# A conditioning projection moved to plain float32 matmuls in 32-column groups, beside a sample attention that has them

## The chip, the cores and the metric

The kernel is one program on one core of a Trainium2 chip. The time is device microseconds of one execution; the figure of merit is the median of several runs. A profiled execution gives the trace.

The engines by their short names: PE is TensorE, whose weight loads are listed apart as PEld; DVE is VectorE, ACT is ScalarE, POOL is GpSimd, and SP is SyncE, which here only issues DMAs, in the order of its queue.

## The reference

One layer of a hybrid encoder for two request groups with shared weights: a prompt of 1024 tokens and 8 samples of 16 tokens each, all float32, width 1024.

```python
def _adaln(c, w_ada, b_ada):                      # w_ada: 1024 x 9216
    return jnp.split(jax.nn.silu(c) @ w_ada + b_ada, 9, axis=-1)

def _layer(x, c, mixer_fn, w_ada, b_ada, ...):
    sh1, sc1, gt1, sh2, sc2, gt2, sh3, sc3, gt3 = _adaln(c, w_ada, b_ada)
    x = x + 0.5 * gt1[:, None, :] * _swiglu(_modulate(x, g_ffn1, sh1, sc1), w_up1, w_down1)
    m, states = mixer_fn(_modulate(x, g_mix, sh2, sc2))
    x = x + gt2[:, None, :] * m
    x = x + 0.5 * gt3[:, None, :] * _swiglu(_modulate(x, g_ffn2, sh3, sc3), w_up2, w_down2)
    return _rms(x, g_final), states
```

`_modulate(x, g, shift, scale)` is `_rms(x, g) * (1 + scale) + shift`; `_swiglu` has an inner width of 2816. The mixer projects to q, k, v, forget logits and a convolution pair, runs a forgetting attention on 8 heads of 64 (the samples with 256 cached keys each) and a causal convolution of 31 taps, and projects back. The conditioning vectors `c` are few: one for the prompt and eight for the samples, so `_adaln` is a product of 9 x 1024 by 1024 x 9216. Its nine results (shift, scale and gate of three sublayers) are what the change is about.

## The kernel before, in words

All 1152 tokens are kept transposed in SBUF (features on the 128 partitions, tokens along the free axis), in three chunks of 384 tokens; chunk 2 holds the samples in its last 128 columns.

Numbers of float32 go through PE split in two: a value rounded to `float32r` (hi) and the rest (lo), and `mm3` makes three matmuls of them (hi·hi, hi·lo, lo·hi; lines 478 to 480). The weights come as blocks of 512 KB through `Stream` (`ws`): SP loads a block (`raw`, three buffers), ACT rounds it (`wh`, L117), POOL or DVE subtracts (`wl`, L118).

PE's order is written by hand: within `manual_schedule` its instructions run in the order of the program. The other engines' order, and that of SP's queue, is the planner's.

`ffn` goes over units: U (up: two matmul groups `ua` and `ub` of 24 matmuls in `glu_mm`, then the SwiGLU on ACT and DVE) and D (down: eight groups `d`). Each unit runs over the three chunks. `tick()` is called after `ua`, after `ub` and after each half of a down; what was put off with `defer(n, f)` runs n ticks later. In this way small pieces of work are placed between the matmuls of the FFN.

The conditioning is one of them. `w_ada` is taken as 18 column blocks j of 512 (block j is half of one of the nine results); each has 8 steps of 128 rows (k). The stationary operand is the conditioning (9 vectors), the moving one the rows of `w_ada` (128 x 512), and the result (9 x 512) collects in a PSUM bank `pa`. When a block is complete, ACT copies it out (`ev`, L355), `ada_tail` transposes it in four pieces to feature layout (`pt`), and DVE adds the bias (`mods`, L365) and prepares scale and gate (`finish_mod`).

- Blocks are computed in the order 2, 0, 3, 1, 4, 5, 6, ..., 17 (`ADA_ORDER`): first halves of scale and shift of the first FFN, then the second halves, the gate, and then the rest.
- The first two blocks are plain float32 matmuls (L348, stationary operand `cst32`, 9 columns wide). The other 16 are split: ACT rounds 128 x 512 (`ahi`, L335), DVE or POOL subtracts (`alo`, L336), and two matmuls (L351 and L352) use an 18 column wide stationary operand `cst` with the hi and lo parts of the conditioning side by side. The two results of 9 rows are added on DVE (L368).
- Rows come by `ada_load` (256 KB each, three buffers `araw`), and for the first four blocks six of eight k in one load of 1.5 MB (`ada_bulk`), into room that the normalised input `hh`/`hl` takes later.
- The first two blocks run ahead of the FFN. The FFN then starts with chunk 0 on half of its features, in four banks `ub` side by side; `first(k)` is called between its pieces. `first(1)` transposes the x of chunk 1 into place, `first(4)` runs blocks three and four and the norm of the second half, `first(5)` and `first(6)` the norm statistics of chunk 1 (`stats_b`: `nb`, L429) and its normalisation, `first(7)` places chunk 2, and `first(9)` starts `ada_tick`, which from then on makes one step each tick (two for a stretch of blocks six and seven).
- PSUM has eight banks; in this part of the kernel one pool of eight serves all of it, `pa` too.

The sample attention later in the kernel already has plain float32 matmuls in 32-column groups: `s_b` (L1054, bank `sS`) and `s_d` (L1077, `sO`) put four small products in the four 32-partition groups of one bank:

```python
for p in range(4):
    rows = slice(32 * p, 32 * p + 32)
    pe.matmul(b[rows, :LK], lhsT=bd[:, rows], rhs=KT[:, p, :], start=True, stop=False)
```

Of the kernel before, what the change touches and what calls it, by code (L numbers as in the profile page):

```python
# [17 lines left out]
P = 128  # L18
D = 1024
KD = D // P  # L20
# [23 lines left out]
def trunk_layer(  # L44
# [18 lines left out]
    const = ctx.enter_context(tc.tile_pool(name="const", bufs=1, side="left"))  # L63
# [14 lines left out]
    def defer(n, f):  # L78
        pending.append([n, f])
# [49 lines left out]
    def kpn(ap):  # L129
        return ap.rearrange("(k p) n -> p k n", p=P)  # L130
# [53 lines left out]
    mods = const.tile([P, 72, 9], F32, name="mods")  # L184
    amod = const.tile([P, 3, KD, 9], F32, name="amod")
    hgate = const.tile([P, 2, KD, 9], F32, name="hgate")
    cst = const.tile([P, KD, 18], F32R, name="cst")
    xt = [xp.tile([P, KD, C], F32, name=f"x{c}") for c in range(NC3)]
    bada = vecs[:, 0:72]
    gnorm = [vecs[:, 72 + 8 * i:80 + 8 * i] for i in range(3)]  # L190
# [6 lines left out]
    nfsd = dram.tile([H, NS, LK], F32, name="nfsd")  # L197

    mps, ps = open_pool("ps", "left", space=PSUM)
    nb = 8  # L200

    def bank(name="b"):
        return ps.tile([P, 512], F32, tag="b", name=name, bufs=nb)
# [15 lines left out]
    cst32 = pro.tile([P, KD, 9], F32, tag="cst32", name="cst32")  # L219
    xin = {}  # L220

    def load_x(i):
# [28 lines left out]
    def T(out, in_):  # L251
        pe.transpose(out, in_, ident[:in_.shape[0], :in_.shape[0]])
# [3 lines left out]
    for k in range(KD):  # L256
        T(pc[:, k * 9:(k + 1) * 9], cwide[:, k * P:(k + 1) * P])
    pcv = pc[:, :72].rearrange("p (k s) -> p k s", s=9)
    act.copy(cst[:, :, 0:9], pcv)
    dve.tensor_copy(cst32, pcv)  # L260
    dve.tensor_sub(cst[:, :, 9:18], pcv, r32(cst[:, :, 0:9]))

    def place_vec():
        pv = bank("pv")
        T(pv[:, :80], vrow)
        act.copy(vecs[:, :80], pv[:, :80])
# [18 lines left out]
                dve.tensor_copy(dst, src)  # L285


    ADA_ORDER = [2, 0, 3, 1, 4, 5] + list(range(6, 18))
# [12 lines left out]
    KORD = [6, 7, 0, 1, 2, 3, 4, 5]  # L301

    def ada_load(n):
        if n < 18 * KD and n not in ada_raw:
            j, k = ADA_ORDER[n // KD], KORD[n % KD]
            t = adp.tile([P, 512], F32, tag="araw", name="araw", bufs=3)
            sp.dma_start(t, w_ada[0, k * P:(k + 1) * P, j * 512:(j + 1) * 512])
            ada_raw[n] = t

    def ada_bulk(g, tag):  # L310
        j = ADA_ORDER[g]
        for n in range(g * KD, g * KD + 2):
            ada_load(n)
        t = hp.tile([P, 6, 512], F32, tag=tag, name="abulk")
        sp.dma_start(t, kpn(w_ada[0, :6 * P, j * 512:(j + 1) * 512]))
        for k in range(6):
            ada_raw[g * KD + 2 + k] = t[:, k]

    FULL = 2
    NA = 18 * KD  # L320
    ada_q, ada_t, ada_n, ada_p = [], [], [0], [None]

    def ada_split():
        n = ada_n[0]
        ada_n[0] += 1
        if n >= 4 * KD - 2:
            for q in range(max(n, 4 * KD), n + 3):
                ada_load(q)
        raw = ada_raw.pop(n)
        if n < FULL * KD:  # L330
            ada_q.append((n, raw, None))
            return
        hi = adp.tile([P, 512], F32R, tag="ahi", name="ahi", bufs=3)
        lo = adp.tile([P, 512], F32R, tag="alo", name="alo", bufs=3)
        act.copy(hi, raw)  # L335
        (pool_e if n >= 4 * KD else dve).tensor_sub(lo, raw, r32(hi))  # L336
        ada_q.append((n, hi, lo))

    def ada_mm():
        n, hi, lo = ada_q.pop(0)  # L340
        j, k = ADA_ORDER[n // KD], KORD[n % KD]
        first, last = n % KD == 0, n % KD == KD - 1
        if first:
            ada_p[0] = bank("pa")
        pa = ada_p[0]
        if lo is None:
            r = 9
            pe.matmul(pa[:r, :], lhsT=cst32[:, k, :], rhs=hi, start=first, stop=last)  # L348
        else:
            r = 18  # L350
            pe.matmul(pa[:r, :], lhsT=cst[:, k, :], rhs=hi, start=first, stop=False)  # L351
            pe.matmul(pa[:r, :], lhsT=cst[:, k, :], rhs=lo, start=False, stop=last)  # L352
        if last:
            ev = tmp(512, "ev", r)
            act.copy(ev, pa[:r, :])  # L355
            ada_t.append((j, r, ev))

    def ada_tail():
        j, r, ev = ada_t.pop(0)
# [3 lines left out]
        ptv = pt[:, :4 * r].rearrange("p (i s) -> p i s", s=r)  # L363
        dst = mods[:, 4 * j:4 * j + 4, :]
        dve.tensor_tensor(  # L365
            dst, ptv[:, :, 0:9], bada[:, 4 * j:4 * j + 4].unsqueeze(2).to_broadcast([P, 4, 9]), ALU.add)
        if r == 18:
            dve.tensor_tensor(dst, ptv[:, :, 9:18], dst, ALU.add)  # L368
        finish_mod(j)

    def ada_step():
        if ada_t:
            ada_tail()
        if ada_n[0] < NA:
            ada_split()
            if len(ada_q) > 2:
                ada_mm()
        elif ada_q:
            ada_mm()
        return ada_n[0] < NA or ada_q or ada_t  # L380

    def ada_blocks(n):
        for _ in range(n):
            ada_split()
            if len(ada_q) > 1:
                ada_mm()

    def ada_close():
        while ada_q:
            ada_mm()  # L390
        ada_tail()

    def ada_group():
        ada_blocks(KD)
        while ada_q:
            ada_mm()

    def run(gen, n):
# [188 lines left out]
            after(c)  # L587


    ada_bulk(0, "hh1")  # L590
    ada_bulk(1, "hl1")
    for i in range(3):
        place_x(i, xin[i])
    stats_a(0)
# [8 lines left out]
    ada_tail()  # L603
# [17 lines left out]
    def first(k):  # L621
        if k == 0:
            norm_apply(0, 0, (0, 1))
        elif k == 1:
            for i in range(3, 6):
                place_x(i, xin[i])
        elif k == 4:
            ada_blocks(KD + 2)
            ada_tail()
            ada_blocks(KD - 2)  # L630
            ada_close()
            norm_apply(0, 0, (2, 3))
            stats_a(1)
        elif k == 5:
            stats_b(1)
        elif k == 6:
            stats_c(1)
            norm_apply(1, 0)
        elif k == 7:
            for i in range(3):  # L640
                place_x(6 + i, x2[:, i])
        elif k == KD + 1:
            load_small()
            ada_tick()
# [28 lines left out]
    mps, ps = open_pool("ps1", "left", space=PSUM)  # L673
    nb = 6
# [186 lines left out]
    for cb, (c0, n) in enumerate(QKV):  # L861
# [3 lines left out]
        for tt in [8] + list(range(8)):  # L865
# [10 lines left out]
            rows = slice(tt * P, (tt + 1) * P)  # L876
            t = sample_rows(cb) if tt == 8 and cb > 1 else tmp(256, "qkv")
# [359 lines left out]
    for n in range(len(stages) + LAG):  # L1237
        q = {k: [] for k in "SBXY"}
        if n < len(stages):
            h, j = stages[n]  # L1240
# [9 lines left out]
        if n >= LAG:  # L1250
            h, j = stages[n - LAG]
# [14 lines left out]
    mps, ps = open_pool("ps3", "left", space=PSUM)  # L1266
    nb = 8
# [23 lines left out]
    mh, hp = open_pool("h2", "left")  # L1291
# [98 lines left out]
```

## Time and profile before

| | |
|---|---|
| median of 3 runs | 2399.08 us (2397.36 to 2401.82) |
| profiled execution, its own time | 2399.03 us |
| its span in the trace | 2397.3 us |
| mean granted PE clock | 0.989 |
| instructions | 34979 |

How to read the profile. Busy time of an engine counts its work, not its waits or the issuing of DMAs. Matmuls are pipelined: a record's length runs from its start to the end of its results, so that lengths overlap and the distance from start to start says what one costs. In the timeline a row is a run of like instructions: start, length from the first start to the last end, engine, line, operation, out<-in, stationary and moving shapes, and in brackets the idle time before it and what ended it. In the table of stretches each row is a part of the span. The rows of a tile give the shortest, middle and longest duration in ns, then the first and the last start.

### The profile page before, as it was taken

How to read it: one execution, taken by the hardware profiler on the slowest of the kernel's cores; microseconds unless marked ns; L12 is line 12 of the kernel's file. 1: busy time of each engine (PE TensorE's matmuls, PEld its weight loads, DVE VectorE, ACT ScalarE, POOL GpSimd, SP SyncE). 2: the span in 40 equal slices, each digit the busy share in tenths (PEclk: the TensorE clock that was granted, in tenths of full speed). 3: DMA queues.
4: the chain of work that ended last, by engine and by line, in shares of the span. 5: the costliest groups of instructions: out<-in, count | busy, mean ns of one | idle time of the engine just before them, and what ended most of it. 6: DMA issues, size and time to landing. Idle time of an engine off the chain costs nothing.

```text
span 2397.3 us, 34979 instructions
## 1 busy us (share of the span) xinstructions
PE 2335.4 (97%) x13971; PEld 2236.0 (93%) x13971; DVE 1277.2 (53%) x2381; ACT 729.5 (30%) x1567; POOL 680.8 (28%) x535
## 2 busy tenths in 40 slices
PE   8899999999999999999989999999999999999998
PEld 4899999999999999999987779999999999999997
DVE  5542543343344436799978887744442344333345
ACT  5533222222111113412658764431111111111112
POOL 2254444443211211131536651112112121121220
PEclk9899999999999999999999999999999999999999
DMA  8133333332111111114233331111111111111102
GB/s 296 57 115 96 95 94 99 93 89 66 45 44 36 47 42 36 37 54 140 89 94 126 93 96 36 45 36 51 38 36 53 36 45 44 36 53 36 37 26 79
DMA packets 176699, 165.81 MB, mean 69 GB/s; under 512 B 11135, under 2 KB 143147, under 8 KB 176529
## 3 DMA queue, kind: packets, MB, share of 16 engines
q1 hardware_dynamic: 176537, 163.58, 22.5%
q8 instruction: 110, 1.80, 0.3%
q14 instruction: 52, 0.43, 0.1%
HBM read 147.10 MB, written 16.68 MB: 68 GB/s over the span
## 4 chain that ended last, share of the span: by engine, by line
PE 84%; DVE 10%; ACT 2%; DMA 2%; issue 1%; POOL 0%; SPq 0%; DVEq 0%; ACTq 0%; POOLq 0%
PE ub L479 8%; PE ub L478 8%; PE ub L480 8%; PE ua L479 8%; PE ua L480 8%; PE ua L478 8%; PE d L480 8%; PE d L478 8%; PE d L479 8%; DVE cv L728 4%; DVE acc L729 1%; DMA nfb<-nfd 1%; PE pa L351 1%; PE pa L352 1%; PE wo L480 1%
## 5 line engine op out<-in xcount | busy, mean ns | idle before, releaser
L118 POOL TENSOR_TENSOR wl<-raw,wh 128x1024 fp32r<-128x1024 f32 (+1 forms) x152 | 368.5, 2432 | 1246.3 <-ACT wh L117 1237.9
L517 DVE TENSOR_TENSOR g<-ub,sg 128x384 f32<-128x384 f32 x132 | 73.6, 558 | 764.5 <-PE ub L480 735.8
L478 PE MATMUL ub<-hh,wh 128*128 128x384 f32 x1168 | 397.7, 341 | 2.5 <-ACT hh L462 2.5
L479 PE MATMUL ub<-hl,wh 128*128 128x384 f32 x1168 | 397.5, 340 | 1.9 <-DVE hl L463 1.9
L480 PE MATMUL ub<-hh,wl 128*128 128x384 f32 x1168 | 397.0, 340 | 0.0
L478 PE MATMUL ua<-hh,wh 128*128 128x384 f32 x1136 | 382.0, 336 | 3.7 <-ACT hh L473 3.3
L479 PE MATMUL ua<-hl,wh 128*128 128x384 f32 x1136 | 381.7, 336 | 0.2
L480 PE MATMUL ua<-hh,wl 128*128 128x384 f32 x1136 | 381.3, 336 | 0.0
L485 DVE SCALAR_TENSOR_TENSOR x<-d,hgate,x 128x384 f32<-128x384 f32 (+1 forms) x528 | 296.1, 571 | 134.0 <-PE d L480 127.9
L117 ACT CAST wh<-raw 128x1024 fp32r<-128x1024 f32 (+1 forms) x160 | 165.6, 1050 | 652.4 <-issue 332.6
L478 PE MATMUL d<-gh,wh 128*128 128x384 f32 x1056 | 357.7, 339 | 3.7 <-DVE t L461 3.6
L480 PE MATMUL d<-gh,wl 128*128 128x384 f32 x1056 | 358.1, 339 | 0.0
L479 PE MATMUL d<-gl,wh 128*128 128x384 f32 x1056 | 357.3, 338 | 0.0
L478 PEld LDWEIGHTS ub<-hh,wh 128*128 128x128 f32 x1168 | 221.2, 189 | 7.6 <-ACT hh L462 2.7
L479 PEld LDWEIGHTS ub<-hl,wh 128*128 128x128 f32 x1168 | 221.2, 189 | 4.3 <-DVE hl L463 2.7
L478 PEld LDWEIGHTS ua<-hh,wh 128*128 128x128 f32 x1136 | 214.4, 189 | 9.5 <-ACT hh L473 4.4
L480 PEld LDWEIGHTS ub<-hh,wl 128*128 128x128 f32 x1168 | 221.2, 189 | 0.0
L479 PEld LDWEIGHTS ua<-hl,wh 128*128 128x128 f32 x1136 | 214.3, 189 | 2.9 <-DVE hl L474 1.0
L336 POOL TENSOR_TENSOR alo<-araw,ahi 128x512 fp32r<-128x512 f32 x112 | 149.0, 1335 | 237.2 <-ACT ahi L335 237.2
L480 PEld LDWEIGHTS ua<-hh,wl 128*128 128x128 f32 x1136 | 214.4, 189 | 0.0
L478 PEld LDWEIGHTS d<-gh,wh 128*128 128x128 f32 x1056 | 199.4, 189 | 8.8 <-DVE t L461 3.9
L521 DVE TENSOR_TENSOR gl<-g,gh 128x384 fp32r<-128x384 f32 x132 | 164.6, 1247 | 68.8 <-ACT gh L520 68.8
(274 smaller groups left out, 3634.8 us busy)
## 6 DMA issues: line engine op xcount, KB each, us to landing
raw<-in_w_up_dram SPq DMA_DIRECT2D x88, 512.0 KB
araw<-in_w_ada_dram SPq DMA_DIRECT2D x120, 256.0 KB
raw<-in_w_down_dram SPq DMA_DIRECT2D x44, 512.0 KB
raw<-in_w_in_dram SPq DMA_DIRECT2D x18, 512.0 KB
abulk<-in_w_ada_dram SPq DMA_DIRECT2D x4, 1536.0 KB
out_dram<-yo SPq DMA_DIRECT2D x18, 256.0 KB
out_dram<-qkv SPq DMA_DIRECT2D x34, 128.0 KB
room<-in_cache_k_dram SPq DMA_DIRECT2D x8, 512.0 KB
```

What stands on the lines that cost most here:

```text
L117: act.copy(hi[:, :a * b], raw)
L118: self.sub.tensor_sub(lo[:, :a * b], raw, r32(hi[:, :a * b]))
L336: (pool_e if n >= 4 * KD else dve).tensor_sub(lo, raw, r32(hi))
L351: pe.matmul(pa[:r, :], lhsT=cst[:, k, :], rhs=hi, start=first, stop=False)
L352: pe.matmul(pa[:r, :], lhsT=cst[:, k, :], rhs=lo, start=False, stop=last)
L478: pe.matmul(out, lhsT=wh, rhs=mh_, start=first, stop=False)
L479: pe.matmul(out, lhsT=wh, rhs=ml_, start=False, stop=False)
L480: pe.matmul(out, lhsT=wl, rhs=mh_, start=False, stop=last)
L485: dve.scalar_tensor_tensor(xs[:, :n], b[:, :n], gate[:, dt, 0:1], xs[:, :n], ALU.mult, ALU.add)
L517: dve.tensor_tensor(g32, pb[:, :C], sg, ALU.mult)
L521: dve.tensor_sub(gl[:, cs], g32, r32(gh[:, cs]))
L728: dve.scalar_tensor_tensor(cv if j < CW - 1 else acc[ct][:, :SEQ], u0, w, cv, ALU.mult, ALU.add)
```

## The change

- All of the conditioning becomes plain float32. The split operand `cst`, the rounding and the subtraction (`ada_split`) and the second addition go.
- The stationary operand `cst32` is 32 columns wide: the nine vectors, and zeros.
- Column blocks are computed in sets: two sets of two blocks, one of two (the gate) and three of four (`SETS`). A step takes one k for all blocks of its set; block i of the set writes partitions 32i to 32i+31 of `pa`. There are 6 x 8 = 48 steps in place of 144.
- `pa` gets a bank of its own, and the pool keeps seven.
- A load brings the rows of the whole set: 128 x 1024 or 128 x 2048 (the first two sets, whose blocks aren't next to each other, by two loads), with two buffers. `ada_step`, `ada_blocks` and `ada_close` go.
- At the start, two steps of set 0 run ahead of the vector transposes and `stats_b`, and six behind them. `first(4)` runs set 1. `ada_tick` makes one step each tick for set 2 and the first step of each set, and otherwise one each fourth tick.
- `ada_tail` transposes 64 or 128 rows in four pieces, once for a set.

```diff
-    cst = const.tile([P, KD, 18], F32R, name="cst")
-    nb = 8
+    nb = 7
...
+    cst32 = adp.tile([P, KD, 32], F32, tag="cst32", name="cst32")
-    act.copy(cst[:, :, 0:9], pcv)
-    dve.tensor_copy(cst32, pcv)
-    dve.tensor_sub(cst[:, :, 9:18], pcv, r32(cst[:, :, 0:9]))
+    dve.memset(cst32, 0.0)
+    dve.tensor_copy(cst32[:, :, 0:9], pcv)
...
+    SETS = [[2, 0], [3, 1], [4, 5]] + [list(range(j, j + 4)) for j in range(6, 18, 4)]
+    STEPS = [(s, k) for s in range(len(SETS)) for k in KORD]
     def ada_load(n):
-            t = adp.tile([P, 512], F32, tag="araw", name="araw", bufs=3)
-            sp.dma_start(t, w_ada[0, k * P:(k + 1) * P, j * 512:(j + 1) * 512])
+        t = adp.tile([P, 2048], F32, tag="araw", name="araw", bufs=2)
+        if js == list(range(js[0], js[0] + len(js))):
+            sp.dma_start(t[:, :512 * len(js)], rows[:, 512 * js[0]:512 * (js[-1] + 1)])
+        else:
+            for i, j in enumerate(js):
+                sp.dma_start(t[:, 512 * i:512 * (i + 1)], rows[:, 512 * j:512 * (j + 1)])
...
     def ada_mm():
+            ada_p[0] = ps.tile([P, 512], F32, tag="pa", name="pa", bufs=1)
-            pe.matmul(pa[:r, :], lhsT=cst[:, k, :], rhs=hi, start=first, stop=False)
-            pe.matmul(pa[:r, :], lhsT=cst[:, k, :], rhs=lo, start=False, stop=last)
+        for i, raw in enumerate(ada_raw.pop(n)):
+            pe.matmul(pa[32 * i:32 * i + 32, :], lhsT=cst32[:, k, :], rhs=raw, start=first, stop=last)
+        if n >= 2 * KD - 2:
+            ada_load(n + 2)
         if last:
-            ev = tmp(512, "ev", r)
-            act.copy(ev, pa[:r, :])
+            ev = tmp(512, "ev", 32 * len(js))
+            act.copy(ev, pa[:32 * len(js), :])
...
-    ada_group()
+    for _ in range(2):
+        ada_mm()
     place_vec()
     stats_b(0)
-    ada_tail()
-    ada_group()
+    for _ in range(6):
+        ada_mm()
     stats_c(0)
     ada_tail()
     ws.split(2)
-    ada_bulk(2, "hh2")
-    ada_bulk(3, "hl2")
+    ada_bulk(1, ("hh2", "hl2"))
...
         elif k == 4:
-            ada_blocks(KD + 2)
+            ada_group()
             ada_tail()
-            ada_blocks(KD - 2)
-            ada_close()
...
     def ada_tick():
-        if 5 * KD <= ada_n[0] < 6 * KD + 4:
-            ada_step()
-        if ada_step():
+        if ada_ev:
+            ada_tail()
+        if ada_n[0] < len(STEPS):
+            ada_mm()
+            defer(1 if ada_n[0] < 3 * KD or ada_n[0] % KD == 0 else 4, ada_tick)
+        elif ada_ev:
             defer(1, ada_tick)
```

More of the change, by code (lines that the diff above doesn't have):

```diff
@@ L218, in trunk_layer @@
     vrow2 = adp.tile([28, P], F32, tag="vrow2", name="vrow2")
-    cst32 = pro.tile([P, KD, 9], F32, tag="cst32", name="cst32")
     xin = {}
@@ L285, in place_x @@
                 dve.tensor_copy(dst, src)
-    ADA_ORDER = [2, 0, 3, 1, 4, 5] + list(range(6, 18))
+    SETS = [[2, 0], [3, 1], [4, 5]] + [list(range(j, j + 4)) for j in range(6, 18, 4)]
+    KORD = [6, 7, 0, 1, 2, 3, 4, 5]
+    STEPS = [(s, k) for s in range(len(SETS)) for k in KORD]
     def finish_mod(j):
@@ L300, in trunk_layer @@
     ada_raw = {}
-    KORD = [6, 7, 0, 1, 2, 3, 4, 5]
     def ada_load(n):
-        if n < 18 * KD and n not in ada_raw:
-            j, k = ADA_ORDER[n // KD], KORD[n % KD]
-            t = adp.tile([P, 512], F32, tag="araw", name="araw", bufs=3)
-            sp.dma_start(t, w_ada[0, k * P:(k + 1) * P, j * 512:(j + 1) * 512])
-            ada_raw[n] = t
-    def ada_bulk(g, tag):
-        j = ADA_ORDER[g]
+        if n >= len(STEPS) or n in ada_raw:
+            return
+        g, k = STEPS[n]
@@ new lines, in ada_load @@
+        js = SETS[g]
+        t = adp.tile([P, 2048], F32, tag="araw", name="araw", bufs=2)
+        rows = w_ada[0, k * P:(k + 1) * P]
+        if js == list(range(js[0], js[0] + len(js))):
[3 more added lines that the diff above has]
+                sp.dma_start(t[:, 512 * i:512 * (i + 1)], rows[:, 512 * j:512 * (j + 1)])
+        ada_raw[n] = [t[:, 512 * i:512 * (i + 1)] for i in range(len(js))]
@@ L312, in ada_bulk @@
+    def ada_bulk(g, tags):
         for n in range(g * KD, g * KD + 2):
             ada_load(n)
-        t = hp.tile([P, 6, 512], F32, tag=tag, name="abulk")
-        sp.dma_start(t, kpn(w_ada[0, :6 * P, j * 512:(j + 1) * 512]))
-        for k in range(6):
[L317 to L323, printed above, removed]
+        ts = []
+        for j, tag in zip(SETS[g], tags):
+            t = hp.tile([P, 6, 512], F32, tag=tag, name="abulk")
+            sp.dma_start(t, kpn(w_ada[0, :6 * P, j * 512:(j + 1) * 512]))
+            ts.append(t)
+        for k in range(6):
+            ada_raw[g * KD + 2 + k] = [t[:, k] for t in ts]
@@ L324, in ada_split, with ada_mm @@
+    ada_n, ada_p, ada_ev = [0], [None], []
+    def ada_mm():
         n = ada_n[0]
         ada_n[0] += 1
[L326 to L341, printed above, removed]
+        g, k = STEPS[n]
+        js = SETS[g]
         first, last = n % KD == 0, n % KD == KD - 1
         if first:
-            ada_p[0] = bank("pa")
+            ada_p[0] = ps.tile([P, 512], F32, tag="pa", name="pa", bufs=1)
         pa = ada_p[0]
[L346 to L352, printed above, removed]
+        for i, raw in enumerate(ada_raw.pop(n)):
+            pe.matmul(pa[32 * i:32 * i + 32, :], lhsT=cst32[:, k, :], rhs=raw, start=first, stop=last)
@@ L353, in ada_mm @@
+        if n >= 2 * KD - 2:
+            ada_load(n + 2)
         if last:
-            ev = tmp(512, "ev", r)
-            act.copy(ev, pa[:r, :])
-            ada_t.append((j, r, ev))
+            ev = tmp(512, "ev", 32 * len(js))
+            act.copy(ev, pa[:32 * len(js), :])
+            ada_ev.append((js, ev))
     def ada_tail():
-        j, r, ev = ada_t.pop(0)
+        js, ev = ada_ev.pop(0)
+        r = 32 * len(js)
         pt = bank("pt")
@@ L362, in ada_tail @@
             T(pt[:, i * r:(i + 1) * r], ev[:, i * P:(i + 1) * P])
[L363 to L372, printed above, removed]
-            ada_tail()
[L374 to L391, printed above, removed]
+        for i, j in enumerate(js):
+            ptv = pt[:, :4 * r].rearrange("p (i s) -> p i s", s=r)[:, :, 32 * i:32 * i + 9]
+            dve.tensor_tensor(
+                mods[:, 4 * j:4 * j + 4, :], ptv, bada[:, 4 * j:4 * j + 4].unsqueeze(2).to_broadcast([P, 4, 9]),
+                ALU.add)
+            finish_mod(j)
     def ada_group():
-        ada_blocks(KD)
-        while ada_q:
+        for _ in range(KD):
             ada_mm()
@@ L587, in ffn @@
             after(c)
-    ada_bulk(0, "hh1")
-    ada_bulk(1, "hl1")
+    ada_bulk(0, ("hh1", "hl1"))
     for i in range(3):
@@ L599, in trunk_layer @@
     ws.dma(3)
-    ada_group()
+    for _ in range(2):
+        ada_mm()
     place_vec()
     stats_b(0)
-    ada_tail()
-    ada_group()
+    for _ in range(6):
+        ada_mm()
     stats_c(0)
```

## Prediction

> **What bounds the kernel now.** The page first: which engine is full.
>
> ```profile
> span 2397.3 us, 34979 instructions
> ...
> PE 2335.4 (97%) x13971; PEld 2236.0 (93%) x13971; DVE 1277.2 (53%) x2381; ACT 729.5 (30%) x1567; POOL 680.8 (28%) x535
> ```
>
> TensorE (PE) is busy for 97% of the span. An average hides stages, so next comes the table of stretches over the part in which the conditioning runs. Its columns: length, then busy time (and instructions) of PE, weight loads, VectorE, ScalarE, GpSimd, then granted clock, DMA share and GB/s.
>
> ```profile
> 62.00:130.00 68.00, 63.31 (x329) 57.69 (x329) 37.13 (x67) 37.65 (x68) 22.88 (x14) 0.90 0.25 74
> 130.00:600.00 470.00, 470.00 (x2639) 440.86 (x2638) 189.90 (x321) 123.88 (x211) 208.12 (x132) 1.00 0.31 91
> 600.00:800.00 200.00, 200.00 (x1147) 200.00 (x1146) 74.35 (x133) 32.55 (x50) 38.41 (x16) 1.00 0.14 43
> ```
>
> From 130 to 600 us PE has no idle time at all, at full clock. Whatever time an instruction holds PE there is time of the kernel, and GpSimd (208 us) and ScalarE (124 us) are cover only. Ahead of 130 us PE does wait, so the two regions are costed apart: the steady part by PE time, the front by its waits. Then the rows that touch the conditioning's accumulator pa:
>
> ```profile
> L351 PE MATMUL pa<-ahi,cst x128: 387/395/408, 41.8 to 591.8; 128*18 128x512 f32 x128
> ...
> L348 PE MATMUL pa<-abulk,cst x24: 592/592/597, 13.6 to 26.4; 128*9 128x512 f32 x24
> ...
> L348 PE MATMUL pa<-araw,cst x8: 592/592/597, 11.7 to 21.3; 128*9 128x512 f32 x8
> ```
>
> L351 has 128 executions, and L352 as many beside it: 16 column blocks x 8 k, a hi and a lo matmul each. The first two blocks are plain float32 (L348). There the trace shows 24+8 records for 2 x 8 matmuls, so a plain float32 matmul is two records.
>
> **Steady part, what goes.** The matmul timeline around 200 us (start, length, ...):
>
> ```profile
> 200.17 0.40 PE L351 MATMUL pa<-ahi,cst 128*18 128x512 f32 x1
> 200.41 0.40 PE L352 MATMUL pa<-alo,cst 128*18 128x512 f32 x1
> 200.64 0.34 PE L478 MATMUL ua<-hh,wh 128*128 128x384 f32 x1
> ...
> 209.47 0.40 PE L351 MATMUL pa<-ahi,cst 128*18 128x512 f32 x1
> ...
> 214.10 0.40 PE L351 MATMUL pa<-ahi,cst 128*18 128x512 f32 x1
> ...
> 218.89 0.41 PE L252 MATMUL pt<-ident,ev 18*128 18x18 f32 x4
> 219.23 0.41 PE L351 MATMUL pa<-ahi,cst 128*18 128x512 f32 x1
> ```
>
> The lengths overlap; starts count. A pair holds PE from 200.17 to 200.64: 0.47 us. From pair to pair 4.63 us pass without a tail (209.47 to 214.10) and 5.13 with one (214.10 to 219.23): a tail (four transposes) costs 0.50 us. Between 200.64 and 209.47 lie 48 FFN matmuls and one pair, so those are (8.83 - 0.47) / 48 = 0.174 us apart. Of the 18 blocks, 14 run after the front: 14 x 8 x 0.47 = 52.6 us of pairs and 14 x 0.50 = 7.0 us of tails, 59.6 together.
>
> **Steady part, what comes.** 32 steps (set 2 two column blocks wide, sets 3 to 5 four wide, 8 k each) and 4 tails. A step's price has no row at 512 columns side by side. The sample attention has the form at other sizes:
>
> ```profile
> 1264.39 0.86 PE L1077 MATMUL sO<-room,room 128*32 128x128 f32 x24
> ...
> 1405.13 0.60 PE L252 MATMUL pT<-ident,T 128*128 128x128 f32 x4
> 1405.67 0.67 PE L1054 MATMUL sS<-room,room 128*32 128x272 f32 x8
> 1406.27 0.72 PE L1055 MATMUL sS<-room,room 40*128 40x272 f32 x2
> 1406.97 0.38 PE L1207 MATMUL po<-ph,Vs 128*128 128x256 f32 x1
> ```
>
> And the plain ones of 512 columns in the front, beside other rows of the front used further down:
>
> ```profile
> 13.56 5.32 PE L348 MATMUL pa<-abulk,cst 128*9 128x512 f32 x12
> ...
> 21.70 5.31 PE L348 MATMUL pa<-abulk,cst 128*9 128x512 f32 x12
> ...
> 34.97 2.78 PE L252 MATMUL xb<-ident,xin 128*128 128x128 f32 x24
> ...
> 51.35 0.41 PE L352 MATMUL pa<-alo,cst 128*18 128x512 f32 x1
> ...
> 54.41 0.44 PE L478 MATMUL ub<-hh,wh 128*128 128x384 f32 x1 [1.56 <-ACT hh L462]
> ...
> 61.71 0.80 PE L429 MATMUL nb<-ones,s 128*128 128x1 f32 x6 [2.32 <-DVE s L420]
> 62.38 0.43 PE L478 MATMUL ub<-hh,wh 128*128 128x384 f32 x1
> ...
> 65.75 0.52 PE L480 MATMUL ub<-hh,wl 128*128 128x384 f32 x1
> ```
>
> Twelve records in 5.31 us, the last 0.59 long: (5.31 - 0.59) / 11 = 0.43 us each, 0.86 us for one plain float32 matmul of 512 columns. Scaled to 272 columns a record is 0.228 us. The eight records of sS are four matmuls; one after the other they would take 8 x 0.228 = 1.82 us, and the next instruction starts 0.60 us after them (1405.67 to 1406.27). So four go side by side, for 2 x 0.228 = 0.46 plus 0.14. The twelve matmuls of sO are through in 0.86 us, where 24 x 0.107 = 2.6 would be the serial time. That each has its own moving operand makes no difference: these have too.
>
> What surrounds the group counts as well. Before it: four transposes cost 4 x 2.78 / 24 = 0.46, and 0.54 us pass (1405.13 to 1405.67): 0.08 to enter. Behind it: L1055's two records take 0.70 (1406.27 to 1406.97) for 0.46 of work: 0.24, part of it that instruction's own next change, so I take half, 0.12. A step then costs 0.86 + 0.08 + 0.14 + 0.12 = **1.20 us**, whether two or four wide; bounds 0.86 (no switching cost) and 1.32 (all 0.24). 32 x 1.20 = 38.4 us (27.5 to 42.2). A tail now transposes 64 or 128 rows: 4 x 0.116 = 0.46 for the four, plus the 0.16 of today's 0.50 that isn't the four (218.89 to 219.23 is 0.34): 0.62, 4 x 0.62 = 2.5. Together 40.9 us. **Gain of the steady part: 59.6 - 40.9 = 18.7 us** (14.9 to 29.6).
>
> The Trainium skill has a rule that gives less: TensorE: Matmul & The Clock Gate (Part 3, Measured speedup vs the span model) lets a packed group cost one matmul plus some 4 ns for each further tile, which by estimate is 0.87 us a step and 28 us for the 32, so 2360 for the whole. The Trainium skill also says, in TensorEngine Tiling (Array Packing), Key Properties, that a change of tiling mode drains the engine, which speaks against this change, since each step enters and leaves the mode alone between two full-width matmuls; the trace agrees with that one (0.60 us where 0.46 is work).
>
> **Off PE.** 116 rounding casts of ScalarE and 128 subtractions (16 on VectorE, 112 on GpSimd) go; in the steady part they cover nothing and gain nothing. DMA bytes are the same. The loads become 8 KB rows, two buffers ahead; a step comes each fourth tick (a tick is one `ua`, `ub` or half a down), about 4 x 24 x 0.174 = 17 us for 1 MB, where the table shows 91 GB/s and a share of 0.31. In set 2 it comes every tick, 512 KB in about 5.4 us with two steps of lead. I cost this at nothing; without the cover each late step would stop PE, since its order is written by hand. Seven banks instead of eight with pa apart: today pa holds one of the eight for most of the time, so nothing, except where x is transposed in `first(1)`: four banks are held by ub and one by rb, three are free now, two then. I take one bank's four transposes (4 x 0.116) as the delay, -0.5 us. After 600 us a bank is truly lost, with PE at 200 of 200 us; nothing.
>
> **Front.** Here the start is set by bytes. Sizes from the page, rates from the table of stretches:
>
> ```profile
> araw<-in_w_ada_dram SPq DMA_DIRECT2D x120, 256.0 KB
> ...
> abulk<-in_w_ada_dram SPq DMA_DIRECT2D x4, 1536.0 KB
> ```
> ```profile
> 0.00:13.60 13.60, 8.04 (x37) 6.22 (x38) 3.14 (x9) 5.54 (x8) 1.08 (x8) 1.00 0.82 295
> 13.60:34.00 20.40, 18.24 (x65) 7.39 (x65) 10.37 (x20) 12.50 (x21) 7.57 (x4) 1.00 1.08 347
> ```
>
> Block one's bulk lands at 13.56, after 13.6 x 295 = 4.0 MB. Set 0 needs both bulks: 0.26 + 1.57 MB more, at 347 GB/s 5.3 us, 18.9 us. Six double steps of 0.86 end at 24.1, where block two ends now at 21.70 + 5.31 = 27.0. The norm statistics (stats_b) stand after two steps, inside the wait. Set 1 needs all of 13.7 MB (x of two chunks 3.1, four raw blocks 2.1, 8.4 of conditioning, small ones): 13.6 + 9.7 / 0.347 = 41.6 us, so its last six steps end at about 47.1 with the switch. Now the last pair ends at 51.8 and the FFN goes on at 54.41, 2.65 later; then 2.9 later (scale and shift come in one tail), 50.0. **Gain 4.4 us.** Next: at 61.71 PE has waited 2.32 us for the second chunk's sum of squares, which stood behind the casts and subtractions on ScalarE and VectorE, and afterwards matmuls start 0.31 us apart (62.38 to 65.75 for 11) instead of 0.174: 1.5 us of reduced clock. With the casts gone the squares run under set 1. **Gain 3.8 us.** Third, the wait for chunk 2's normalised input:
>
> ```profile
> 94.44 0.40 PE L352 MATMUL pa<-alo,cst 128*18 128x512 f32 x1
> 97.90 0.69 PE L478 MATMUL ua<-hh,wh 128*128 128x384 f32 x1 [3.06 <-ACT hh L473]
> ...
> 107.21 0.39 PE L351 MATMUL pa<-ahi,cst 128*18 128x512 f32 x1
> ```
>
> It loses 3.2 us ahead of 97.90 and 9.3 - 24 x 0.174 = 5.1 behind it. The VectorE chain is late next as before; but two steps of 1.20 now stand in the wait instead of two pairs, and GpSimd no longer subtracts beside it: I take 2.4 (0 to 8.3). Front: 4.4 + 3.8 + 2.4 - 0.5 = **10.1 us** (0 to 16).
>
> **Sum.** 18.7 + 10.1 = 28.8 us off the profiled execution's 2399.03 us (span 2397.3, 1.7 around it; the median of the runs is 2399.08, the same): **2370 us**.
>
> **Rivals.**
> A. *The front stays.* VectorE's chain and the bytes fix it. For: VectorE is busy 37 of 68 us there and the DMA share is 1.08 up to 34 us. Against: the 2.32 us wait follows from removed work. 2399 - 18.7 = 2380.
> B. *Switching is free* at 512 columns (weights for the second half are loaded early): 0.86 a step, 10.9 less: 2359. Against: 0.14 us inside the sS group. This is also what the span model of the Trainium skill gives (TensorE: Matmul & The Clock Gate, Part 3).
> C. *Late rows.* SP's queue is in order; a load that waits for its buffer holds up the raw FFN weights behind it, and PE stops. For: SP waits on slots today as well. Against: PE never idles there. The price is the wait per step; from 28.8 / 32 = 0.9 us a step on there is no gain, at 1.5 us the time is 2418.
> D. *No concurrency.* The change doesn't do what it says: 24 x 4 x 0.86 + 8 x 2 x 0.86 = 96.3 us of matmuls in place of 27.5, with the gains of the sum otherwise kept 2370 + 69 = 2439. Break-even is a step of (59.6 + 10.1 - 2.5) / 32 = 2.1 us. Against: sS and sO.
>
> **How the numbers follow.** Forecast 0.63, A 0.20, B 0.08, C 0.05 (0.02 still faster, 0.01 the same, 0.02 slower), D 0.04. Runs differ by about 0.2%, some 5 us, which is what can be told from no change: faster 0.93, same 0.01, slower 0.06. The range takes in B at the bottom and A with the dear step (2380 + 3.8) at the top, with 2 to 3 us for order changes elsewhere: 2358 to 2387.
>
> **What would show it.** Right: no L335/L336 groups; from pa step to pa step in the steady part, ub's last start to ua's first start is 1.2 us plus 0.174, with x4 or x8 records; PE without idle time from 110 to 600 us; set 0's last record near 24 us, the FFN resuming near 50, nb without a wait. Wrong: records of a step 0.43 apart one after the other (D); PE waiting for araw's DMA or for wl (C); the second chunk's statistics still late (A).

## The result and the profile after

The changed kernel takes 2375.18 us in the median of 4 runs (2371.12 to 2375.61); the kernel before beside it takes 2398.22 us (2395.76 to 2401.82). The ratio is 0.9899 [0.9882, 0.9916], 23 us less. Its profiled execution is the fastest of the four (2371.12 us); against the profiled execution of before the span is 27.9 us shorter. A second set of runs of the same program on another chip (the last experiment) gave 2376.2 us and a span of 2374.1 us. The forecast was 2370 us in 2358 to 2387.

From the page: span, and busy time of each engine.

```profile
span 2369.4 us, 34222 instructions
...
PE 2301.1 (97%) x13923; PEld 2206.7 (93%) x13923; DVE 1240.5 (52%) x2349; ACT 654.3 (28%) x1426; POOL 532.9 (22%) x423
```

PE has lost 34 us of busy time and POOL 148, and the share of PE is again 97%. The table of stretches, with the two of the front added:

```profile
12.00:30.00 18.00, 12.11 (x44) 5.70 (x40) 6.52 (x14) 8.94 (x15) 4.67 (x2) 0.81 1.10 354
30.00:62.00 32.00, 26.40 (x133) 19.74 (x133) 12.44 (x24) 12.93 (x24) 5.05 (x2) 0.89 0.75 262
62.00:130.00 68.00, 63.99 (x336) 52.70 (x335) 35.38 (x68) 30.76 (x54) 9.59 (x4) 0.95 0.40 124
130.00:600.00 470.00, 470.00 (x2728) 444.70 (x2727) 176.63 (x328) 69.25 (x107) 81.63 (x34) 1.00 0.27 86
```

From 130 to 600 us PE still never idles, so no load of the wide rows came late. ACT falls from 124 to 69 us and POOL from 208 to 82 there, and less than 1 us is won by that, as experiment e2 will show. From 12 to 30 us the granted clock is 0.81. Now one step in the steady part, in the timeline of PE:

```profile
158.88 0.34 PE L448 MATMUL d<-gh,wl 128*128 128x384 f32 x1
159.14 1.06 PE L341 MATMUL pa<-araw,cst 128*32 128x512 f32 x8
160.14 0.44 PE L446 MATMUL d<-gh,wh 128*128 128x384 f32 x1
160.42 0.34 PE L447 MATMUL d<-gl,wh 128*128 128x384 f32 x1
```

A step's cost is read from the start ahead of it to the second start behind it, less two of the ordinary distances: 160.42 - 158.88 - 2 x 0.174 = 1.19 us. Over the steady part it is 1.196 to 1.201 us four blocks wide and 1.183 two wide. Eight records of 0.43 us are through in that time: the blocks do run side by side, at the forecast price of 1.20. In parts: the first record starts 0.26 us behind the matmul ahead of it in place of 0.174 (0.09 to enter), the group holds PE for 1.00 us in place of 0.86 (0.14), and the matmul behind it for 0.28 in place of 0.174 (0.11 to leave). The forecast had 0.08, 0.14 and 0.12.

Where the time went, by first starts of the same matmul in three traces (the changed kernel twice):

| stretch | before | after | after, second trace |
|---|---|---|---|
| start to matmul 145 of `ub` | 107.67 | 107.27 | 105.00 |
| from there to matmul 1001 of `ub` | 504.66 | 479.47 | 479.47 |
| to the end of the first FFN (matmul 1701 of `ua`) | 415.89 | 411.12 | 411.73 |
| to matmul 1201 of `z` | 199.19 | 199.12 | 199.13 |
| to the first `wo`: the attention stage | 199.38 | 203.18 | 207.46 |
| to the end of the span | 970.5 | 969.2 | 971.3 |

Matmul 1001 of `ub` stands behind the last matmul of the conditioning in every trace (592.0, 511.8 and 509.5 us in these three). In the first row the changed kernel has done six steps by then (7.1 us of PE), the kernel before four pairs (1.9 us); the front proper has gained 0.4 + 5.2 = 5.6 us, in the second trace 7.9. At matmul 1001 of `ub` it is 25.6 and 27.9 us ahead, against 28.8 forecast. Behind that the sum meets two things that it did not contain: 4.8 and 4.2 us more won at the end of the first FFN, and 3.8 and 8.1 us lost in the attention stage.

### The profile page after: what moved, and what is told of

Read it like the earlier page. It is cut to its first block, busy times and chain, and to the rows that moved or that the text cites. A ratio compares the mean times of both kernels' runs of the same rounds, so it can differ in the third digit from the quotient of the medians.

```text
span 2369.4 us, 34222 instructions
## 1 busy us (share of the span) xinstructions
PE 2301.1 (97%) x13923; PEld 2206.7 (93%) x13923; DVE 1240.5 (52%) x2349; ACT 654.3 (28%) x1426; POOL 532.9 (22%) x423
## 4 chain that ended last, share of the span: by engine, by line
PE 83%; DVE 11%; DMA 2%; ACT 2%; issue 1%; POOL 0%; DVEq 0%; SPq 0%; ACTq 0%; POOLq 0%
PE ub L446 8%; PE ub L447 8%; PE ub L448 8%; PE ua L446 8%; PE ua L447 8%; PE ua L448 8%; PE d L446 8%; PE d L448 8%; PE d L447 8%; DVE cv L696 4%; PE pa L341 2%; DMA nfb<-nfd 1%; DVE acc L697 1%; PE wo L446 1%; PE wo L447 1%
## 5 line engine op out<-in xcount | busy, mean ns | idle before, releaser
L447 PEld LDWEIGHTS d<-gl,wh 128*128 128x128 f32 x1056 | 198.8, 188 | 0.0
L448 PEld LDWEIGHTS d<-gh,wl 128*128 128x128 f32 x1056 | 198.6, 188 | 0.0
```

The lines of the kernel that those rows point to most:

```text
L447: pe.matmul(out, lhsT=wh, rhs=ml_, start=False, stop=False)
L448: pe.matmul(out, lhsT=wl, rhs=mh_, start=False, stop=last)
```

## The experiments

Three things were to be settled. **The step:** is its excess over 0.86 us the price of leaving and re-entering TensorE's whole-array form (M), or does it come from something else: the plain float32 format between the rounded ones (D), the number of blocks, or 32 columns as such? **The gain:** does it come from the PE time of the steps, or from relief of ACT, POOL and the DMA queue, or from the bank? **The front:** what kept its forecast gain away: PE's standstill and the lowered clock, or the place of the squares on ACT?

**Two steps, one behind the other** (e1). Two steps in one visit enter and leave once.

```diff
             ada_mm()
-            defer(1 if ada_n[0] < 3 * KD or ada_n[0] % KD == 0 else 4, ada_tick)
+            ada_mm()
+            defer(1 if ada_n[0] % KD == 0 else 2 if ada_n[0] < 3 * KD else 8, ada_tick)
```

> The changed kernel with two steps made one behind the other, half as often (each 2nd tick in set 2, each 8th later); the same matmuls, loads and tails. Theory 1 (the steady part is PE time; 0.34 us of a step's 1.20 is entering and leaving the 32-column mode): 16 of 32 entries go, 16 x 0.34 = 5.4 us less, a double step takes 2 x 0.86 + 0.34 = 2.06 us, the median about 2370. Rival (the gain is the relief of ScalarE, GpSimd and the DMA queue, and a step's price is the matmuls alone): no change, 2375.

2374.52 us (2371.25 to 2378.78), ratio 0.9891 [0.9876, 0.9906]. A double step costs 2.053 to 2.060 us where it is not held up, so 0.34 us are saved by each entry spared. But in this schedule the first double step of a set comes one tick after the last of the set before, and its rows are late:

```profile
234.18 1.07 PE L341 MATMUL pa<-araw,cst 128*32 128x512 f32 x8
236.15 1.06 PE L341 MATMUL pa<-araw,cst 128*32 128x512 f32 x8 [0.91 <-DMA araw<-in_w_ada_dram]
```

The first double steps of sets 3, 4 and 5 take 5.6, 3.1 and 3.0 us. The saving was given back to a wait for DMA: the time is the rival's number, but the mechanism holds and the schedule was wrong.

**Two steps, evenly spaced** (e5). The same with eight ticks at the set borders as well.

```diff
     def ada_tick():
+        ada_mm()
+        ada_mm()
         if ada_ev:
-            ada_tail()
+            defer(1, ada_tail)
         if ada_n[0] < len(STEPS):
-            ada_mm()
-            defer(1 if ada_n[0] < 3 * KD or ada_n[0] % KD == 0 else 4, ada_tick)
-        elif ada_ev:
-            defer(1, ada_tick)
+            defer(2 if ada_n[0] < 3 * KD else 8, ada_tick)
```

> Two steps behind one another as in the first experiment, but evenly spaced over the borders of the sets too (8 ticks, from set 2 to set 3 8 as well; the tail one tick behind the set), so that each pair of loads has its time to land. Theory 1 (0.34 us of a step is entering and leaving): every double step 2.06 us, none with a wait of 1 to 3 us at a border, 16 entries fewer, 5 us less than the changed kernel in the trace by the end of the conditioning. Rival (switching isn't the price; the double steps of the first experiment gained nothing): equal to the changed kernel.

2368.25 us (2367.41 to 2371.91), ratio 0.9864 [0.9847, 0.988]. No step of the steady part waits. One of the 16:

```profile
182.94 0.34 PE L448 MATMUL ub<-hh,wl 128*128 128x384 f32 x1
183.21 1.92 PE L341 MATMUL pa<-araw,cst 128*32 128x512 f32 x16
185.07 0.45 PE L446 MATMUL ua<-hh,wh 128*128 128x384 f32 x1
185.35 0.34 PE L447 MATMUL ua<-hl,wh 128*128 128x384 f32 x1
```

185.35 - 182.94 - 0.35 = 2.06 us, against 2 x 1.20. From matmul 145 to matmul 1001 of `ub` it takes 475.23 us, 4.2 less than the changed kernel in either trace. Thirteen of the sixteen entries spared lie in that stretch; at 0.34 they would be 4.4.

**One block a step** (e2). From block 6 on there is nothing side by side: 96 steps in place of 24. All else stays; the casts do not come back.

```diff
-    SETS = [[2, 0], [3, 1], [4, 5]] + [list(range(j, j + 4)) for j in range(6, 18, 4)]
+    SETS = [[2, 0], [3, 1], [4, 5]] + [[j] for j in range(6, 18)]
...
-            defer(1 if ada_n[0] < 3 * KD or ada_n[0] % KD == 0 else 4, ada_tick)
+            defer(1, ada_tick)
```

> The changed kernel without matmuls side by side from block 6 on: each of the 12 blocks is a set of its own, 96 steps of one plain float32 matmul in the first 32 columns, one each tick, 12 tails. Theory 1: 96 x 0.86 = 82.6 us for 24 x 1.20 = 28.8, and 9 more tails of 0.5: 58 us more than the changed kernel, span about 2430, if a group of 32 columns alone does not switch; 96 x 1.20 = 115 and 91 more, about 2463, if it does. Rival (the relief of ScalarE and GpSimd is the gain): these are relieved just the same here, so about 2375.

2459.77 us (one run), span 2458.1: 88.7 us more than the changed kernel's. ACT, POOL and the queue are relieved here just the same, and the kernel is far slower than before: the relief is not the gain. Read in the same way and added up one by one, the steps and tails between matmul 145 and matmul 1001 of `ub` hold PE for 57.1 us in the kernel before, 32.8 in the changed one and 120.0 here. That is 24.3 less and 87.2 more; the stretch itself changed by 25.2 and 87.7. So less than 1 us of the steady part's gain is anything but the PE time of steps and tails. A single step:

```profile
138.81 0.34 PE L448 MATMUL ua<-hh,wl 128*128 128x384 f32 x1
139.07 1.05 PE L341 MATMUL pa<-araw,cst 128*32 128x512 f32 x2
140.05 0.44 PE L446 MATMUL ub<-hh,wh 128*128 128x384 f32 x1
140.33 0.34 PE L447 MATMUL ub<-hl,wh 128*128 128x384 f32 x1
```

140.33 - 138.81 - 0.35 = 1.17 us (1.176 to 1.181 over the part): one block costs within 0.02 us what four cost. 72 more steps at 1.18 are 85 us, and nine tails come on top. The excess of 0.3 us does not need a second block.

**Nine columns** (e7). As e2, with a stationary operand of nine columns, as in the front of the kernel before.

```diff
-            pe.matmul(pa[32 * i:32 * i + 32, :], lhsT=cst32[:, k, :], rhs=raw, start=first, stop=last)
+            if len(js) == 1:
+                pe.matmul(pa[:9, :], lhsT=cst32[:, k, 0:9], rhs=raw, start=first, stop=last)
...
```

> As the experiment with one block a step (96 steps from block 6 on), but with a stationary operand of 9 columns, as the kernel before has for its first two blocks, and 9 rows of the bank. Theory 1 (32 columns in a bank's quarter change the array's mode, 9 columns as in the kernel before do not): a step costs 0.86 and not 1.18, 96 x 0.32 = 31 us less than with 32 columns, span about 2427. Rival (float32 between float32r costs 0.32 in itself, whatever the columns): span 2458.

2458.59 us (one run), span 2456.9. The step costs 1.157 us, the same excess:

```profile
140.77 0.34 PE L452 MATMUL ua<-hh,wl 128*128 128x384 f32 x1
141.04 1.03 PE L342 MATMUL pa<-araw,cst 128*9 128x512 f32 x2
141.99 0.44 PE L450 MATMUL ub<-hh,wh 128*128 128x384 f32 x1
142.27 0.34 PE L451 MATMUL ub<-hl,wh 128*128 128x384 f32 x1
```

That missed: a narrow operand was thought to stay in the whole-array form. Either nine columns already take a 32-column part, or plain float32 between rounded operands costs the 0.3 us by itself. The next run separates these.

**Full width** (e9). As e2, with `cst32` padded by zeros to 128 columns; the format is still plain float32.

```diff
...
+                pe.matmul(pa[:, :], lhsT=cst128[:, k, :], rhs=raw, start=first, stop=last)
...
```

> As the experiment with one block a step (96 steps from block 6 on), but with a stationary operand of 128 columns (the nine vectors and zeros), so that the plain float32 matmul uses the whole array like the FFN's float32r matmuls around it, and writes the whole bank. Theory M (the 0.3 us around a step is the change from the whole array to a 32-column part of it and back; the nine columns of the last experiment count as a 32-column part too): a step costs 0.86 to 0.9, 96 x 0.28 = 27 us less than with nine columns, span about 2430. Theory D (plain float32 between float32r costs it, whatever the columns): 1.16 to 1.25 a step, span 2457 to 2465. For D speaks that the kernel before has 18 float32r columns, a pair 0.47 us in all, with no such excess.

2434.71 us (one run), span 2433.0, 25.1 less than e2; between matmul 145 and matmul 1001 of `ub` it is 28.8 less for 96 steps, each 0.857 to 0.861 us:

```profile
142.94 0.34 PE L453 MATMUL ub<-hh,wl 128*128 128x384 f32 x1
143.12 1.02 PE L343 MATMUL pa<-araw,cst 128*128 128x512 f32 x2
143.57 0.73 PE L451 MATMUL ua<-hh,wh 128*128 128x384 f32 x1
144.15 0.34 PE L452 MATMUL ua<-hl,wh 128*128 128x384 f32 x1
```

144.15 - 142.94 - 0.35 = 0.86: exactly two records of 0.43, with no excess. It is not the format alone. With a plain float32 operand of 32 or of nine columns, about 0.32 us go on entering and leaving; at 128 columns none do, and no width between was run. The Trainium skill says in TensorEngine Tiling (Array Packing), Key Properties, that a change of the tiling mode drains TensorE; these rows agree and give the price here, 1.18 - 0.86 = 0.32 us for a visit. They show the price and that it is paid by the visit, but not that the time is a drain. What stays open is why the kernel before shows no such excess: its pairs with an 18 column operand in the rounded format cost 0.47 us for two matmuls of 512 columns.

**A bank of its own** (e4). The kernel before, with `pa` in a bank apart and seven banks for the rest.

```diff
-    nb = 8
+    nb = 7
...
+            ada_p[0] = ps.tile([P, 512], F32, tag="pa", name="pa", bufs=1)
```

> The kernel before, with the conditioning's accumulator in a bank of its own and seven banks for the rest, nothing else of the change. Theory 1: no change in the steady part, within 2 us, 2398. Rival (part of the gain, that behind the first FFN, comes from the banks): 2 to 5 us less, and the waits for d and rb near 950 us are different from before.

2403.15 us, ratio 1.0008 [0.9999, 1.0017]. The steady part is as before. Matmul 145 of `ub` comes 2.6 us later, and most of that is lost ahead of `first(7)`, which places the x of chunk 2. Its first transposes, in e4 and then in the kernel before:

```profile
70.52 1.03 PE L252 MATMUL xb<-ident,x 128*128 128x128 f32 x8
```
```profile
68.57 2.12 PE L252 MATMUL xb<-ident,x 128*128 128x128 f32 x16
```

They start 1.95 us later; from 66 to 70 us the granted clock is 0.61 in place of 0.98. The first `ua` behind them starts at 77.38 us in place of 75.14, so `first(7)` itself takes 6.86 us in place of 6.57: 0.3 us for the bank. The rest lies within what two traces of one program differ by in the front (2.3 us, see e11). In sum none of the gain is the bank's.

**Squares early** (e3). `stats_a(1)`, the sum of squares of chunk 1, is called ahead of set 1 instead of behind it.

```diff
         elif k == 4:
+            stats_a(1)
             ada_group()
             ada_tail()
             norm_apply(0, 0, (2, 3))
-            stats_a(1)
```

> The changed kernel with the squares of chunk 1 (stats_a(1)) called ahead of set 1 and not behind the norm that follows it. Theory 1 (order on ScalarE holds the squares back, not its load): the wait of 2.1 us ahead of nb and the reduced clock behind it go, nb comes some 4 us earlier, and 2 to 4 us of it reach the end: 2372. Rival (VectorE's chain for chunk 2 sets the time of the front): nb comes earlier, chunk 2 starts where it did, 2375.

2370.0 us (2366.18 to 2374.33), ratio 0.9866 [0.9849, 0.9882]. The squares now run in ACT's idle time during set 1 and `nb` has no wait. ACT, then PE:

```profile
39.73 0.90 ACT L382 ACTIVATE acc<-x 128x768 f32<-128x768 f32 x1
40.48 2.35 ACT L385 ACTIVATE sq<-x 128x768 f32<-128x768 f32 x3
...
50.24 0.58 ACT L346 COPY ev<-pa 64x512 f32<-64x512 f32 x1 [7.41 <-PE pa L341]
```
```profile
57.48 0.90 PE L397 MATMUL nb<-ones,s 128*128 128x1 f32 x6
```

`nb` comes 2.4 us earlier than in the changed kernel, and matmul 145 of `ub` 3.7 us earlier (103.60), a lead that is the same at matmul 1001 (583.07 against 586.74). Against the second trace of the changed kernel all three are 1.4 us.

**A busy front** (e6). 16 products of the identity with itself while PE would wait for `stats_b`, and 8 more ahead of the FFN. They compute nothing that is used.

```diff
+    def idle_mm(n):
+        b = bank("idle")
+        for _ in range(n):
+            pe.matmul(b[:, :P], lhsT=ident, rhs=ident, start=True, stop=True)
...
+    idle_mm(16)
...
+    idle_mm(8)
```

> The changed kernel with 16 idle matmuls (128 wide, identity by identity, read by nobody) in the wait ahead of stats_b and 8 behind the first tail, so that PE does not stand still there. Theory 1 (PE stands for 3.9 us ahead of nb, so that set 0 runs its first half at half the clock): set 0's 24 records take 5.3 us and not 8.3, the FFN starts about 2.5 us earlier, and 1 to 3 us of that are left at chunk 2. Rival (the rows of set 0 land late and the matmuls wait for them): 8.3 us as before.

2376.03 us, ratio 0.9896 [0.9881, 0.9911]: no gain on the changed kernel. The front of PE in this run, then the changed kernel's:

```profile
16.65 0.80 PE L397 MATMUL nb<-ones,s 128*128 128x1 f32 x6 [0.28 <-DVE s L388]
...
19.14 5.34 PE L341 MATMUL pa<-abulk,cst 128*32 128x512 f32 x22 [0.71 <-DMA abulk<-in_w_ada_dram]
...
28.13 0.45 PE L446 MATMUL ub<-hh,wh 128*128 128x384 f32 x1 [0.49 <-ACT hh L430]
...
33.33 0.69 PE L447 MATMUL ub<-hl,wh 128*128 128x384 f32 x1 [1.89 <-DVE hl L431]
```
```profile
17.12 1.41 PE L397 MATMUL nb<-ones,s 128*128 128x1 f32 x6 [3.89 <-DVE s L388]
18.46 8.31 PE L341 MATMUL pa<-abulk,cst 128*32 128x512 f32 x24
29.77 0.44 PE L446 MATMUL ub<-hh,wh 128*128 128x384 f32 x1 [1.81 <-ACT hh L430]
...
53.30 0.45 PE L446 MATMUL ub<-hh,wh 128*128 128x384 f32 x1 [1.82 <-ACT hh L430]
59.92 0.80 PE L397 MATMUL nb<-ones,s 128*128 128x1 f32 x6 [2.13 <-DVE s L388]
```

With PE kept busy 22 records take 5.34 us; after a standstill of 3.89 us 24 records take 8.31. Set 0 then ends at 24.5 us instead of 26.8, and the FFN starts 1.6 us earlier. The clock claim is right. But the FFN gains nothing from its earlier start. In the changed kernel ACT makes three `hh` ahead of the first cast of the weights; here the cast, which waits for DMA, comes behind the first `hh`:

```profile
29.38 1.05 ACT L117 CAST wh<-raw 128x1024 fp32r<-128x1024 f32 x1 [1.30 <-DMA raw<-in_w_up_dram]
```

The next two `hl` then run on DVE beside POOL's subtractions and take 2.30 and 2.72 us, where one takes 0.61 without them. PE waits for the first of them (the 1.89 us), and from 34 to 38 us its granted clock is 0.50. In the end `ub` goes on after set 1 at 56.76 us, 3.5 later than in the changed kernel. What a front at full clock would bring with ACT's order unchanged is not shown by this run.

**Combinations.** e8 is e5, e3 and e6 together; e10 is e5 and e3.

```diff
         elif k == 4:
+            stats_a(1)
...
     def ada_tick():
+        ada_mm()
+        ada_mm()
...
```

> The changed kernel with double steps evenly spaced, the squares of chunk 1 ahead of set 1, and the idle matmuls in the front. Theory 1: 5 us (switching) + 3.6 us (squares) + 1 to 3 us (clock) less than the changed kernel, about 10 us, 33 less than the kernel before. Rival (VectorE's chain for chunk 2 takes back what the front wins): 5 us less than the changed kernel.

> The changed kernel with double steps evenly spaced and the squares of chunk 1 ahead of set 1, without the idle matmuls. By the two experiments alone: 5 us and 3.6 us less than the changed kernel by the end of the first FFN, 2 us less than with all three. Rival (the idle matmuls were worth something at the end): 2365 or more.

e8: 2365.3 us (2363.92 to 2367.01), ratio 0.9853 [0.9838, 0.9868]. e10: 2361.47 us (2357.86 to 2364.31), ratio 0.9833 [0.9816, 0.9851]. The two intervals overlap, so whether the idle matmuls cost anything beside the other two is open; they bring nothing. e8 is the expected 10 us below the changed kernel, but not by the expected terms: its front is 5.4 us longer than e10's (matmul 145 of `ub` at 105.36 and 99.93), at the same place as in e6. e10 beats both kernels: on the same chip the changed kernel took 2376.2 us. Of the 14.9 us between the two traces 9.3 lie ahead of matmul 1001 of `ub` (575.16 against 584.47), near the 8.6 expected, and 5.8 in the attention stage, which neither edit touches. In e10 the clock of the stretch from 62 to 130 us is 1.00:

```profile
62.00:130.00 68.00, 63.55 (x349) 54.52 (x349) 31.43 (x62) 29.88 (x53) 9.60 (x4) 1.00 0.32 109
```

**The changed kernel once more** (e11), with no edit, beside e9 and e10.

> The changed kernel once more, beside the last two on the same chip: 2375 and a span of 2369 to 2374 in the trace; the front and the steady part as in its first trace, to 0.3 us. Rival (the first profiled execution was 4 us faster than its timed runs for a reason in the front or the steady part): the difference shows there.

2376.2 us (2373.59 to 2378.59), ratio 0.9895 [0.988, 0.991]; the milestones stand in the table above. The steady part is the same (479.47 us). The front is 1.0 to 2.3 us earlier than in the first trace, where 0.3 was expected at most, and the attention stage 4.3 us longer, with the same program. From 12 to 30 us the granted clock is 0.89 here and 0.81 there. The first execution was not faster in the front or the steady part, so the rival falls. Over all thirteen traces the attention stage, which no experiment touches, takes 199.4 to 207.6 us.

## Why the prediction was right, and which steps failed

**Steady part: right in kind and size.** The price of a step was put at 1.20 us "whether two or four wide", from the groups of the sample attention; 1.183 to 1.201 were measured, and e2 and e9 show that it is 0.86 of work and 0.32 of changing form, as the step said. From matmul 145 to matmul 1001 of `ub` the sum gives: goes 108 pairs x 0.47 and 14 tails x 0.50, comes 26 steps x 1.20 and 4 tails x 0.62, a gain of 24.1 us; measured 25.2 in both traces. A tail alone cost 0.44 us and not 0.62. The 0.12 for leaving was half of a measured 0.24, chosen without a row; that it came out is in part luck. Rival B (0.86 a step) falls, and with it, for a group alone between full-width matmuls, the span model of the Trainium skill (TensorE: Matmul & The Clock Gate, Part 3), which gave 0.87 by estimate. Rival D falls on the eight records in 1.06 us. Rival C falls for the change (no wait in the steady part), but e1 shows how near it lay: one tick between double steps is enough.

**Front: 10.1 us forecast, 5.6 and 7.9 measured.** Rival A (0) is further off, but these steps failed.

- "Six double steps of 0.86 end at 24.1." The rows were there as forecast (the steps start at 18.46 us without a wait), but the set ended at 26.8. "The norm statistics (stats_b) stand after two steps, inside the wait" was taken as free. PE stood still for 3.89 us there, and the matmuls behind it ran slowly: 8.31 us in place of 5.34. In the kernel before, twelve records of the same kind in this place took 5.31 us at full clock.
- "41.6 us, so its last six steps end at about 47.1." The end of set 1 was taken from the bytes. In the changed kernel no step of set 1 waits for its rows:

```profile
43.28 1.91 PE L341 MATMUL pa<-araw,cst 128*32 128x512 f32 x8
45.02 5.32 PE L341 MATMUL pa<-abulk,cst 128*32 128x512 f32 x24
```

  The eight steps run in one piece to 50.34 us, behind the first pieces of the FFN, which hold PE from 29.77 us on for 13.5 us at a granted clock of 0.87 (12.7 us at full clock in the kernel before). So the FFN went on at 53.30 and not at 50.0: 1.1 us won of 4.4. The late end of set 0 alone does not set this time. In nine traces with the same front set 0's last record starts between 24.8 and 26.3 us and the FFN goes on between 52.2 and 53.8, and the one does not follow the other (25.2 and 53.4 in e5).
- "With the casts gone the squares run under set 1." They did not. ACT is idle for 10.34 us and still takes the squares only behind the copy-out:

```profile
50.39 0.58 ACT L346 COPY ev<-pa 64x512 f32<-64x512 f32 x1 [10.34 <-PE pa L341]
...
53.15 0.83 ACT L382 ACTIVATE acc<-x 128x768 f32<-128x768 f32 x1
...
56.14 1.56 ACT L385 ACTIVATE sq<-x 128x768 f32<-128x768 f32 x2
```

  What held them was their place in ACT's order, not a lack of room. `nb` waits 2.13 us where 2.32 had been and nothing was forecast. e3 changes that one call and the wait is gone.
- The bank: "-0.5 us" was put at `first(1)`. In e4 nothing is lost there (12.68 us in place of 12.70 from the FFN's first matmul to the next pair), and 0.3 us at `first(7)`.

Behind `nb` the forecast had 1.5 us for the clock and 2.4 for chunk 2's wait. From `nb` to matmul 145 of `ub`, less the conditioning done in it, 44.1 us became 40.2, 3.8 less, and 5.0 less in the second trace. But it was hardly the wait: PE's idle time there fell from 4.6 to 4.0 us (4.2 in the second trace), while the granted clock rose from 0.85 to 0.93 (0.96).

**Unforeseen.** At the end of the first FFN 4.2 to 4.8 us were won. In the kernel before PE waits 3.31 us there for the norm factor `rh`, which stands behind a square on ACT:

```profile
971.28 0.84 ACT L414 ACTIVATE acc<-x 128x768 f32<-128x768 f32 x1 [2.90 <-DVE x L491]
973.09 0.98 ACT L437 ACTIVATE rh<-ident,r 128x128 fp32r<-128x128 f32 x3 [0.97 <-DVE r L432]
974.13 0.69 PE L444 MATMUL rb<-rh,onesr 128*128 128x384 f32 x1 [3.31 <-ACT rh L437]
```

and in the changed kernel the order is the other way round:

```profile
942.23 0.99 ACT L405 ACTIVATE rh<-ident,r 128x128 fp32r<-128x128 f32 x3 [0.42 <-DVE r L400]
943.13 0.83 ACT L382 ACTIVATE acc<-x 128x768 f32<-128x768 f32 x1
944.03 0.34 PE L412 MATMUL rb<-rh,onesr 128*128 128x384 f32 x1
```

The bank apart is enough for this order: e4, which changes only that, has it too, ACT first and then PE:

```profile
971.04 0.98 ACT L437 ACTIVATE rh<-ident,r 128x128 fp32r<-128x128 f32 x3 [0.38 <-DVE r L432]
971.93 0.83 ACT L414 ACTIVATE acc<-x 128x768 f32<-128x768 f32 x1
```
```profile
970.98 0.69 PE L478 MATMUL ua<-hh,wh 128*128 128x384 f32 x1 [2.70 <-DVE rs L488]
...
978.06 0.34 PE L444 MATMUL rb<-rh,onesr 128*128 128x384 f32 x1
```

`rb` has no wait there either, but PE stands 2.70 us for the residual sum `rs` just ahead, and over the stretch e4 keeps 0.3 us. In the changed kernel that wait is 0.34 us. What makes `rs` earlier there was not tested. The waits are also the smaller part: over the stretch PE's idle time falls from 7.3 us (before and e4) to 6.2, while the granted clock rises from 0.988 to 0.996, and to 0.992 in the second trace. All eleven traces without the casts take 411.1 to 413.1 us here, also e2 with nothing side by side, and the two with them 415.6 and 415.9. So it is neither the packing nor the bank, and the cause of these 4 us is open. The attention stage took 3.8 to 8.1 us back. Its length goes in part with the clock: 199.4 us at a granted clock of 0.98 before, 203.2 at 0.97 and 207.5 at 0.96 in the two traces of the changed kernel. The kernel before has the shortest of all thirteen, and e4, which differs by the bank alone, 203.3 at 0.98. Why the stage varies was not tested, and none of it is put down to the change.

So the number came out partly by luck. The front fell short by 2.2 to 4.5 us, the steady part gave 1.1 more, and two stretches that the sum did not contain gave 4.2 to 4.8 and took 3.8 to 8.1. These errors nearly cancel: 28.8 us forecast, 27.9 between the two traces, 23 between the medians.

## What to carry to other kernels

Small plain float32 products are worth putting side by side where PE is the bound, but their price is paid by the visit: count the visits, make two steps in one, and keep the same lead for the loads as before (0.34 us saved a visit, and all of it lost where rows came 0.9 to 3.5 us late). A wait that work "in front" of an engine seems to cause may be the engine's order instead: look whether the engine is idle ahead of the late instruction, and if so move the piece of work in the program. A pause of PE is paid twice, by itself and by the clock behind it.

## What was not expected of the hardware

- The excess of a visit comes with the width of the stationary operand and not with packing: one block of 32 columns 1.18 us, nine columns 1.157, 128 columns 0.86. For narrow plain float32 operands alone between full-width matmuls, padding to 128 columns saved 28.8 us over 96 steps. The 18 column operand in the rounded format showed no such excess (0.47 us for two); why was not found.
- After 3.89 us without work PE ran 24 records in 8.31 us, and with filling work 22 in 5.34; the granted clock of the stretch is 0.81. The Trainium skill (TensorE: Matmul & The Clock Gate, Part 1) halves the clock after an idle window of about 3.4 us, which agrees with both. Here no single wait of that length is needed: in the kernel before, behind waits of 0.66, 1.56, 0.83 and 2.32 us between 51 and 62 us, the granted clock from 62 to 66 us is 0.59.
- An `hl` on DVE (128x384) takes 0.61 us, and 1.66 to 2.72 us where it runs beside POOL's subtraction (the changed kernel and e6).
- Two traces of one program differ by 4.3 us in one stage of some 205 us and by 2.3 us in the front, more than some of the effects studied here. The steady part is the same to 0.01 us: single edits are best read over a stretch that they alone touch.
